# Stick-breaking attention: later key blocks summed on VectorE before the matmuls, and a later square for the head norm

## Chip, cores and metric

The kernel runs on one core of a Trainium2 chip. The metric is device time in microseconds (us): 2136.33 us, the median of 3 runs (2136.27 to 2136.56). The engines are called PE (TensorE matmul; PEld is its weight load), DVE (VectorE), ACT (ScalarE), POOL (GpSimd) and SP (the queue that issues the loads).

## The reference

Two transformer blocks run over 512 tokens of width 1024, all in float32. The part that the change touches is the attention of the second block, with 16 heads of 64:

```
q = rms_norm(q, q_gain); k = rms_norm(k, k_gain)      # per head
z = q @ k.T / sqrt(64)                                # masked: only keys s < t
log_1m = log_sigmoid(-z)                              # = -softplus(z)
rev_excl[s] = sum of log_1m over keys j with s < j < t
w = exp(log_sigmoid(z) + rev_excl);  o = w @ v
```

So every weight needs the sum of softplus(z) over all keys after its own. Besides, each of the seven mean-square norms (`rms_norm` over the 1024 rows) needs a sum over partitions.

## The kernel before

Tokens lie along the free axis, 512 wide, and features along the 128 partitions. Weights stream from HBM in chunks of 128x1024; ACT rounds each to a high half (L170), DVE subtracts to get the low half (L171), and each product is three matmuls: high x high, high x low, low x high (L193 to L195, function `mm3`). `split` does the same rounding for activations: ACT copies to fp32r (L188), DVE subtracts (L189). One such group of three 512-column matmuls is called a dense step here; for the value projection (`sv_tile`, L786 to L788) a dense step is six 256-column matmuls.

The attention takes two heads at a time, in eight passes called pair 0 to pair 7 here (`stick`). Scores are kept transposed: keys on partitions, queries on the free axis, only the part with query block >= key block. Side A is the first head, side B the second. The four key blocks of a head have 512, 384, 256 and 128 query columns, and `AT` packs both heads into five PSUM banks: A0 and B0 hold block 0 (512 columns), A1 and B1 hold block 1 (384) and block 3 (128), and Z2 holds block 2 of both sides (256 each). For each pair:

- `front` (L886 to L896): score matmuls, and one that adds the mask.
- ACT and DVE turn each bank z into softplus, bank after bank in the order A1, A0, Z2, B1, B0: absolute value (ACT L904, DVE L906), exp and log (ACT L910, L911), max and add (DVE L915). Then `split` makes the high and low part.
- `middle` (L925 to L931), once for each side: the matmuls that add minus the sum of later softplus onto z in PSUM. For each key block j a matrix with minus ones below and on the diagonal (`nlater`) goes onto block j itself, and a matrix of minus ones (`nones`) onto every earlier block; blocks of 128 columns in float32 (L925, two records each), the others with high and low part (L930, L931). They are called the first sums (side A) and the second sums (side B).
- `weights` (ACT L934): exp. `back` (PE L943): weights times values, for the pair before.

Between these stand dense steps of the projections for later pairs, so that PE has work while ACT and DVE work. `Flow` sets the order: `yield n` in `stick` pulls n dense steps from `sb_dense`, and each step advances a counter t; `F.at(d, fn)` emits a function's instructions d counts later; `tick` advances the counter without a dense step. `qk_tile` sends each projected q or k tile through a chain of this kind: evacuate (DVE L811), square (ACT L816), `NORM_LAG` counts later a float32 matmul over each head's 64 rows (`halves`, PE L822, called the head norm matmul), then `rsqrt` (ACT L232, L233, DVE L235 to L237) and a scale (DVE L828).

PE, ACT and SP run their instructions in the order in which the code emits them. The order on DVE and POOL is set when the program is built, by a scheduler with its own estimates, and is then fixed too: each engine works its list from top to bottom.

`Norm.total` (L257) sums the squares of the 1024 features with a matrix of ones: the sum of squares is split, and two fp32r matmuls of 512 columns run on it. It is called seven times, twice of them in `rstd_pair`.

Of the kernel before, what the change touches and what calls it, by code (L numbers as in the profile page):

```python
# [9 lines left out]
F32 = mybir.dt.float32  # L10
I32 = mybir.dt.int32
F32R = mybir.dt.float32r
AF = mybir.ActivationFunctionType
OP = mybir.AluOpType
PSUM = bass.MemoryType.PSUM

P = 128
S = 512
# [62 lines left out]
def block_kernel(ctx: ExitStack, tc: tile.TileContext, a, out):  # L81
    nc = tc.nc
    dve, act, pe, pool = nc.vector, nc.scalar, nc.tensor, nc.gpsimd

    consts = ctx.enter_context(tc.tile_pool(name="consts", bufs=1))
# [7 lines left out]
    def sl(dt=F32):  # L93
        return slots.tile([P, S], dt, name="sl", tag="sl")

    def bank():
        return psum.tile([P, S], F32, name="ps", tag="ps")
# [87 lines left out]
    def split(x):  # L185
        h = sl(F32R)
        l = sl(F32R)
        act.activation(h, x, AF.Copy)  # L188
        dve.tensor_tensor(l, x, h.bitcast(F32), op=OP.subtract)  # L189
        return h, l  # L190
# [25 lines left out]
    ones = cmat[:, 0:P]  # L216
    ident = cmat[:, P:2 * P]
    halves = cmat[:, 2 * P:3 * P]
    nlater = cmat[:, 3 * P:4 * P]
    nones = cmat[:, 4 * P:5 * P]  # L220
# [18 lines left out]
    class Norm:  # L239
# [13 lines left out]

        def total(self):
            ps = bank()
            for i, part in enumerate(split(self.acc)):
                pe.matmul(ps, ones_r, part, start=i == 0, stop=i == 1)  # L257
            return ps

        def rstd(self):  # L260
# [70 lines left out]
    for k in range(KD):  # L331
        xs.append(scaled_split(x[k], gain(G_N1, k)))
        wh, wl = split(lead[k])
        for n in range(4):
            c = slice(n * P, (n + 1) * P)
# [3 lines left out]
        norm.add(x[k])  # L339
    split_ahead()  # L340

    ones_r = consts.tile([P, P], F32R, name="ones_r")
    pool.tensor_copy(ones_r, ones)
    cc = consts.tile([P, KD], F32, name="cc")
    dve.tensor_tensor(cc, gains[:, G_NF * 8:G_NF * 8 + 8], gains[:, G_F1 * 8:G_F1 * 8 + 8], op=OP.mult)
    qg = consts.tile([P, 1], F32, name="qg")
# [15 lines left out]
    F = Flow()  # L362
# [338 lines left out]
    for m in range(KD):  # L701
# [3 lines left out]
        sa, sb = T.pop(T_GA + m), T.pop(T_GB + m)  # L705
# [9 lines left out]
    for m in [W_EARLY] + list(range(W_EARLY)) + list(range(W_EARLY + 1, KD)):  # L715
        if m < W_EARLY:
# [3 lines left out]
            ps = first[m][0]  # L720
        else:
            ps = bank()
# [46 lines left out]
    F = Flow()  # L769
# [31 lines left out]
    def qk_tile(n, which, g):  # L801
# [12 lines left out]
        def second(t):  # L814
            sq = sl()
            act.activation(sq, t, AF.Square)  # L816
            F.at(NORM_LAG, lambda: third(t, sq))

        def third(t, sq):
            pm = bank()  # L820
            state["bank_free"] = F.t + 8
            pe.matmul(pm, halves, sq, start=True, stop=True)  # L822
            F.at(2, lambda: fourth(t, pm))
# [37 lines left out]
    A0, A1, Z2, B1, B0 = range(5)  # L861
    AT = ({0: (A0, 0), 1: (A1, 0), 2: (Z2, 0), 3: (A1, 384)}, {0: (B0, 0), 1: (B1, 0), 2: (Z2, 256), 3: (B1, 384)})
# [6 lines left out]
    nlater_r = consts.tile([P, P], F32R, name="nlater_r")  # L869
    pool.tensor_copy(nlater_r, nlater)  # L870
    nones_r = consts.tile([P, P], F32R, name="nones_r")
# [3 lines left out]
    def stick():  # L875

        def front(n):

            q, k = Q[n], K[n]
            z = [bank() for _ in range(5)]
            started = set()
            for g, sb in ((0, 1), (1, 1), (0, 3), (1, 3), (0, 0), (1, 0), (0, 2)):
                b, c = AT[g][sb]
                pe.matmul(z[b][:, c:c + S - sb * P], k[HALF[g], sb * P:(sb + 1) * P], q[HALF[g], sb * P:],  # L886
                          start=b not in started, stop=True, skip_group_check=True)
                started.add(b)

            b, c = AT[1][2]  # L890
            pe.matmul(z[b][:, c:c + 2 * P], kz[(8 + n) % 3], q[:, 2 * P:], start=False, stop=True, skip_group_check=True)
            for b in (A1, A0, Z2, B1, B0):
                blocks = z[b].rearrange("p (a c) -> p a c", a=4)
                n_ = 1 if b in (A0, B0) else 2
                blocks = blocks[:, 0:1] if n_ == 1 else blocks[:, 0:3:2] if b == Z2 else blocks[:, 0:4:3]
                pe.matmul(blocks, ident_r, hidden_r[:, :n_ * P].rearrange("p (a c) -> p a c", a=n_), start=False,  # L896
                          stop=True, skip_group_check=True)
            return z

        def absolute(z, b):  # L900

            t = sl()
            if b in (A1, B1):
                act.activation(t, z[b], AF.Abs)  # L904
                return t
            dve.tensor_scalar(t.bitcast(I32), z[b].bitcast(I32), 0x7FFFFFFF, None, op0=OP.bitwise_and)  # L906
            return t

        def log_part(t):
            act.activation(t, t, AF.Exp, scale=-1.0)  # L910
            act.activation(t, t, AF.Ln, bias=1.0)  # L911

        def soft(t, z):

            dve.scalar_tensor_tensor(t, z, 0.0, t, op0=OP.max, op1=OP.add)  # L915

        def middle(z, sp, hl, g):
            for j in ((3, 1, 0, 2), (3, 1, 2, 0))[g]:
                bj, cj = AT[g][j]
                w = S - j * P  # L920
                for sb in range(j, -1, -1):
                    b, c = AT[g][sb]
                    dst = z[b][:, c + (j - sb) * P:c + (j - sb) * P + w]
                    if w == P:
                        pe.matmul(dst, nlater if j == sb else nones, sp[bj][:, cj:cj + w], start=False, stop=True,  # L925
                                  skip_group_check=True)
                        continue
                    hi, lo = hl[bj]
                    m = nlater_r if j == sb else nones_r
                    pe.matmul(dst, m, hi[:, cj:cj + w], start=False, stop=True, skip_group_check=True)  # L930
                    pe.matmul(dst, m, lo[:, cj:cj + w], start=False, stop=True, skip_group_check=True)  # L931

        def weights(z, t, b):
            act.activation(t[b], z[b], AF.Exp)  # L934

        def back(n, t):

            po = bank()
            for sb in range(4):
                for g in range(2):  # L940
                    b, c = AT[g][sb]
                    cv = (sb % 2) * 256 + (n % 2) * P + g * 64
                    pe.matmul(po[HALF[g], sb * P:], v[sb // 2][n // 2][:, cv:cv + 64], t[b][:, c:c + S - sb * P],  # L943
                              start=sb == 0, stop=sb == 3)
            pair = split(po)
            F.at(3, lambda: os_.__setitem__(n, pair))

        last = None
        for n in range(KD):
            while n not in K and F.pull(1):  # L950
                pass
            while n not in K:
                F.t += 1
                F.fire()
            z = front(n)
            F.tick(4)
            sp, hl = {}, {}
            order = (A1, A0, Z2, B1, B0)
            for t in range(6):

                for b in order[:2] if t == 0 else order[t + 1:t + 2]:
                    sp[b] = absolute(z, b)
                if t < 5:
                    log_part(sp[order[t]])
                if 1 <= t:
                    soft(sp[order[t - 1]], z[order[t - 1]])
                if 2 <= t < 5:
                    hl[order[t - 2]] = split(sp[order[t - 2]])
                yield 3 if t < 4 else 2
            middle(z, sp, hl, 0)  # L970
            F.tick(4)
            hl[B1] = split(sp[B1])
            yield 1
            hl[B0] = split(sp[B0])
            yield 3
            weights(z, sp, A1)
            weights(z, sp, A0)
            middle(z, sp, hl, 1)
            F.tick(2)
            for b in (B1, Z2, B0):  # L980
                weights(z, sp, b)
            yield 1
            if n:
                while F.t < state["bank_free"] and F.pull(1):
                    pass
                while v[1][(n - 1) // 2] is None and F.pull(1):
                    pass
                back(n - 1, last)
                F.tick(3)
            yield 2  # L990
            last = sp
        yield 7
        back(KD - 1, last)

    F.dense = sb_dense()
    for steps in stick():
        F.pull(steps)
# [7 lines left out]
    for m in [ne] + list(range(KD)):  # L1005
        if m == ne and xs[m] is not None:
            continue
        ps = bank()
        w = SBO_K[m] if m < ne else 0
# [22 lines left out]
ROPE_LAG = 10  # L1032
STACK_LAG = 5
BACK = 3
NORM_LAG = 4
SCALE_LAG = 8
VALUE_LAG = 4
SBO_K = (5, 5, 6, 6, 6)
# [94 lines left out]
```

## Time and profile before

| what | value |
|---|---|
| median of 3 runs | 2136.33 us |
| the profiled execution | 2135.5 us, its span 2133.6 us |
| PE busy | 2110.0 us (99% of the span) |
| DVE, ACT busy | 1090.8 us (51%), 840.8 us (39%) |
| mean granted PE clock | 0.997 of full speed |
| attention of the second block | about 1499 to 1744 us of the span |

Matmuls are pipelined: a record's duration overlaps the next, so the time that a matmul takes from PE is the distance between the starts of two, called its pitch here. On the other engines too an instruction often starts shortly before the one ahead has ended, so their cost in a row is also a pitch. A float32 matmul shows as two records.

### The profile page before, as it was taken

What the parts mean: (1) busy time and instruction counts of PE and PEld (TensorE: products, weight loads), DVE (VectorE), ACT (ScalarE), POOL (GpSimd) and SP (SyncE); (2) the same over time, 40 slices, a digit from 0 to 9 for tenths busy, and PEclk for the clock granted to TensorE, in tenths of its full rate; (3) what the DMA queues carried; (4) which work ended last, traced back from release to release, by engine and by line L of the source; (5) the groups of instructions that cost most, each with busy time, mean ns of one, the idle gap of its engine ahead of it and who ended that gap; (6) DMA issues with size and microseconds to landing.
All of it is one profiled execution on the core that took longest, in us unless ns stands there. A gap on an engine that the chain in (4) does not pass through costs nothing.

```text
span 2133.6 us, 24868 instructions
## 1 busy us (share of the span) xinstructions
PE 2110.0 (99%) x10022; PEld 1742.3 (82%) x10022; DVE 1090.8 (51%) x1607; ACT 840.8 (39%) x1319; POOL 14.4 (1%) x48
## 2 busy tenths in 40 slices
PE   8999999999999999999999999999999999999999
PEld 7888888887788888888887888888777878888887
DVE  6444344699954744444445444344766656444322
ACT  6222222366766542222233222223656644222210
POOL 0000000000000000000000000000000000000000
PEclk9999999999999999999999999999999999999999
DMA  5323333322212333332332223333111113323331
GB/s 173 104 97 99 92 101 109 102 89 75 72 55 65 119 99 99 99 99 82 101 97 96 92 96 99 92 91 98 58 51 58 35 55 128 97 92 97 97 116 54
DMA packets 58562, 193.55 MB, mean 91 GB/s; under 512 B 6928, under 2 KB 7568, under 8 KB 58448
## 3 DMA queue, kind: packets, MB, share of 16 engines
q1 hardware_dynamic: 56736, 188.67, 28.4%
q0 software_dynamic: 640, 2.10, 0.3%
q8 instruction: 78, 1.28, 0.2%
q10 hardware_dynamic: 1072, 1.21, 0.2%
q14 instruction: 36, 0.29, 0.0%
HBM read 189.20 MB, written 2.10 MB: 90 GB/s over the span
## 4 chain that ended last, share of the span: by engine, by line
PE 89%; DVE 6%; ACT 3%; issue 1%; DMA 1%; SPq 0%; ACTq 0%; DVEq 0%
PE ps L193 26%; PE ps L195 26%; PE ps L194 26%; DVE wl L171 1%; PE ps L943 1%; PE ps L886 1%; PE ps L574 1%; PE ps L931 1%; DVE sl L529 1%; PE ps L631 1%; DMA wraw<-in_f_in_dram 1%; PE ps L930 1%; ACT wh L170 1%; PE ps L562 1%; DVE m L527 1%
## 5 line engine op out<-in xcount | busy, mean ns | idle before, releaser
L193 PE MATMUL ps<-sl,wh 128*128 128x512 f32 x2672 | 1053.2, 394 | 0.0
L194 PE MATMUL ps<-sl,wh 128*128 128x512 f32 x2672 | 1041.7, 390 | 0.2
L195 PE MATMUL ps<-sl,wl 128*128 128x512 f32 x2672 | 1041.8, 390 | 0.0
L193 PEld LDWEIGHTS ps<-sl,wh 128*128 128x128 f32 x2672 | 502.6, 188 | 106.6 <-issue 6.0
L194 PEld LDWEIGHTS ps<-sl,wh 128*128 128x128 f32 x2672 | 502.8, 188 | 105.4 <-issue 2.9
L195 PEld LDWEIGHTS ps<-sl,wl 128*128 128x128 f32 x2672 | 502.4, 188 | 105.4
L170 ACT ACTIVATE wh<-wraw 128x1024 fp32r<-128x1024 f32 (+6 forms) x369 | 369.7, 1003 | 514.8 <-issue 248.8
L171 DVE TENSOR_TENSOR wl<-wraw,wh 128x1024 fp32r<-128x1024 f32 (+6 forms) x369 | 427.5, 1160 | 281.0 <-ACT wh L170 280.4
L188 ACT ACTIVATE sl<-sl 128x512 fp32r<-128x512 f32 x160 | 99.6, 627 | 393.4 <-DVE sl L301 387.5
L301 DVE TENSOR_TENSOR sl<-ps,sl 128x512 f32<-128x512 f32 x88 | 60.9, 692 | 270.2 <-PE ps L195 263.9
L189 DVE TENSOR_TENSOR sl<-sl 128x512 fp32r<-128x512 f32 x160 | 110.0, 689 | 69.8 <-ACT sl L188 69.3
L299 DVE TENSOR_TENSOR sl<-ps,sl 128x512 f32<-128x512 f32 x88 | 60.8, 691 | 140.1 <-PE ps L195 139.9
L251 ACT ACTIVATE sl<-x 128x512 f32<-128x512 f32 x42 | 25.8, 627 | 116.4 <-DVE x L324 97.7
L323 DVE SCALAR_TENSOR_TENSOR sl<-ps,sl 128x512 f32<-128x512 f32 x32 | 22.1, 692 | 80.0 <-PE ps L195 80.0
L300 ACT ACTIVATE sl<-sl 128x512 f32<-128x512 f32 x88 | 54.1, 614 | 9.2 <-DVE sl L299 9.2
L548 ACT ACTIVATE sl<-sl,mx 128x128 f32<-128x128 f32 (+3 forms) x64 | 35.7, 558 | 41.6 <-DVE mx L547 41.4
L555 ACT ACTIVATE sl<-sl,sm 128x128 f32<-128x128 f32 (+3 forms) x64 | 35.8, 560 | 25.2 <-DVE sm L554 15.1
L631 PE MATMUL ps<-sl 128*128 128x256 f32 (+2 forms) x176 | 43.4, 328 | 0.8 <-DVE mx L547 0.8
L252 DVE TENSOR_TENSOR sl<-sl 128x512 f32<-128x512 f32 x49 | 33.3, 690 | 18.0 <-ACT sl L251 17.5
L235 DVE SCALAR_TENSOR_TENSOR sl<-sl 128x512 f32<-128x512 f32 x23 | 15.9, 692 | 48.1 <-ACT sl L233 48.0
L631 PEld LDWEIGHTS ps<-sl 128*128 128x128 f32 x176 | 33.2, 189 | 8.6 <-DVE mx L547 1.2
L786 PE MATMUL ps<-wh,sl 128*128 128x256 f32 x128 | 37.8, 295 | 0.0
(143 smaller groups left out, 1338.0 us busy)
## 6 DMA issues: line engine op xcount, KB each, us to landing
wraw<-in_f_in_dram SPq DMA_DIRECT2D x172, 512.0 KB
wraw<-in_f_out_dram SPq DMA_DIRECT2D x64, 512.0 KB
wraw<-in_mix_t_dram SPq DMA_DIRECT2D x34, 512.0 KB
wraw<-in_f_out_dram SPq DMA_DIRECT2D x32, 384.0 KB
wraw<-in_sb_qk_dram SPq DMA_DIRECT2D x16, 512.0 KB
wraw<-in_br_dram SPq DMA_DIRECT2D x16, 256.0 KB
wraw<-in_w_out_dram SPq DMA_DIRECT2D x8, 512.0 KB
wraw<-in_sb_v_dram SPq DMA_DIRECT2D x8, 512.0 KB
```

Source lines behind the costliest of these rows:

```text
L170: act.activation(wh[:, :n], raw[:, :n], AF.Copy)
L171: dve.tensor_tensor(wl[:, :n], raw[:, :n], wh[:, :n].bitcast(F32), op=OP.subtract)
L188: act.activation(h, x, AF.Copy)
L189: dve.tensor_tensor(l, x, h.bitcast(F32), op=OP.subtract)
L193: pe.matmul(ps, wh, xh, start=start, stop=False)
L194: pe.matmul(ps, wh, xl, start=False, stop=False)
L195: pe.matmul(ps, wl, xh, start=False, stop=stop)
L299: dve.tensor_tensor(g, pg, rs, op=OP.mult)
L300: act.activation(g, g, AF.Silu)
L301: dve.tensor_tensor(g, pu, g, op=OP.mult)
L631: pe.matmul(ps[:, :n], q[:, i * P:(i + 1) * P], part[:, :n], start=x_ == 0, stop=x_ == 1)
L786: pe.matmul(dst, hh, wh[:, cl], start=kk == 0 and b == 0, stop=False)
```

## The change

Three things change. `Norm.total` does one float32 matmul on the unsplit sum. `NORM_LAG` goes from 4 to 6. In `stick`, a new function `suffix` adds up the softplus of later key blocks on DVE, in place, once own parts have been split: block 3 onto block 2's columns, and that onto block 1's; both results are split (ACT L922, DVE L923, 256 and 384 wide). `middle` then takes for each block its own part with `nlater` and one total of all later blocks with `nones`. The yields and ticks around the sums change with it.

```diff
         def total(self):
             ps = bank()
-            for i, part in enumerate(split(self.acc)):
-                pe.matmul(ps, ones_r, part, start=i == 0, stop=i == 1)
+            pe.matmul(ps, ones, self.acc, start=True, stop=True)
             return ps
...
-        def middle(z, sp, hl, g):
-            for j in ((3, 1, 0, 2), (3, 1, 2, 0))[g]:
...
+        def suffix(sp, hl, g, out):
+
+            b1, c2 = AT[g][1][0], AT[g][2][1]
+            two, one = sp[Z2][:, c2:c2 + 256], sp[b1][:, :384]
+            dve.tensor_tensor(two[:, P:], two[:, P:], sp[b1][:, 384:], op=OP.add)
+            dve.tensor_tensor(one[:, P:], one[:, P:], two, op=OP.add)
+            for s, w in ((two, 256), (one, 384)):
+                h, l = sl(F32R), sl(F32R)
+                act.activation(h[:, :w], s, AF.Copy)
+                dve.tensor_tensor(l[:, :w], s, h[:, :w].bitcast(F32), op=OP.subtract)
+                out.append((h[:, :w], l[:, :w]))
+
+        def middle(z, sp, hl, later, g):
+            def take(sb, m, m_r, at, parts):
+                b, c = AT[g][sb]
+                w = S - sb * P - at
+                for part in parts:
+                    pe.matmul(z[b][:, c + at:c + at + w], m if len(parts) == 1 else m_r, part, start=False, stop=True,
+                              skip_group_check=True)
+
+            last_block = sp[AT[g][3][0]][:, 384:]
+            for sb in ((3, 1, 0, 2), (3, 1, 2, 0))[g]:
+                b, c = AT[g][sb]
+                own = [last_block] if sb == 3 else [part[:, c:c + S - sb * P] for part in hl[b]]
+                take(sb, nlater, nlater_r, 0, own)
+            take(2, nones, None, P, [last_block])
+            take(1, None, nones_r, P, later[0])
+            take(0, None, nones_r, P, later[1])
...
                 if 2 <= t < 5:
                     hl[order[t - 2]] = split(sp[order[t - 2]])
+                if t == 4:
+                    suffix(sp, hl, 0, sums[0])
                 yield 3 if t < 4 else 2
-            middle(z, sp, hl, 0)
-            F.tick(4)
+            middle(z, sp, hl, sums[0], 0)
+            F.tick(3)
             hl[B1] = split(sp[B1])
             yield 1
+            suffix(sp, hl, 1, sums[1])
+            yield 2
             hl[B0] = split(sp[B0])
-            yield 3
+            yield 2
             weights(z, sp, A1)
             weights(z, sp, A0)
-            middle(z, sp, hl, 1)
+            middle(z, sp, hl, sums[1], 1)
...
-NORM_LAG = 4
+NORM_LAG = 6
```

PE's list, first sums of pair 2, before (`cmat` holds the float32 matrices, `nlater_r` and `nones_r` are their fp32r copies):

```order
L925 MATMUL ps<-sl,cmat 128x128 x4
L930 MATMUL ps<-sl,nlater_r 128x384
L931 MATMUL ps<-sl,nlater_r 128x384
L930 MATMUL ps<-sl,nones_r 128x384
L931 MATMUL ps<-sl,nones_r 128x384
L930 MATMUL ps<-sl,nlater_r 128x512
L931 MATMUL ps<-sl,nlater_r 128x512
L930 MATMUL ps<-sl,nlater_r 128x256
L931 MATMUL ps<-sl,nlater_r 128x256
```

Two more pairs of 256 columns on `nones_r` follow these rows. The same sums in the changed kernel, with the matmul that now follows them:

```order
L931 MATMUL ps<-sl,cmat 128x128
L931 MATMUL ps<-sl,nlater_r 128x384 x2
L931 MATMUL ps<-sl,nlater_r 128x512 x2
L931 MATMUL ps<-sl,nlater_r 128x256 x2
L931 MATMUL ps<-sl,cmat 128x128
L931 MATMUL ps<-sl,nones_r 128x256 x2
L931 MATMUL ps<-sl,nones_r 128x384 x2
L819 MATMUL ps<-sl,cmat 128x512
```

Two float32 matmuls and two of 256 columns (a high and a low part) are gone; the last four now read what `suffix` makes, and a head norm matmul (L819, L822 before) stands right behind. In pair 2's second sums (side B) the order of own blocks is 3, 1, 2, 0 as before, but block 0's 512-column pair now stands ahead of all `nones`.

DVE's list in pair 2 before, from the split of Z2 (`sl_11917`) over that of B1 (`sl_11933`) to that of B0 (`sl_11957`):

```order
L189 TENSOR_TENSOR sl_12006<-sl_11917,sl_12005 128x512
L235 SCALAR_TENSOR_TENSOR sl_12056<-sl_12053 128x512
L236 SCALAR_TENSOR_TENSOR sl_12056<-ps_12034,sl_12056 128x512
L237 SCALAR_TENSOR_TENSOR sl_12052<-sl_12056,sl_12053 128x512
L189 TENSOR_TENSOR sl_12063<-sl_11933,sl_12062 128x512
L828 SCALAR_TENSOR_TENSOR sl_11986<-sl_11986,gains_80,sl_12052 128x512
L189 TENSOR_TENSOR sl_12073<-sl_11957,sl_12072 128x512
```

One `rsqrt` and its scale lie among the three splits. The same place in the changed kernel, first from the split of Z2 (`sl_11906`) to that of B1 (`sl_11922`); A1 is `sl_11882`:

```order
L189 TENSOR_TENSOR sl_11981<-sl_11906,sl_11980 128x512
L912 SCALAR_TENSOR_TENSOR sl_11940<-ps_11858,sl_11940 128x512
L918 TENSOR_TENSOR sl_11906<-sl_11906,sl_11882 128x128
L918 TENSOR_TENSOR sl_11906<-sl_11906,sl_11922 128x128
L919 TENSOR_TENSOR sl_11882<-sl_11882,sl_11906 128x256
L923 TENSOR_TENSOR sl_11987<-sl_11906,sl_11986 128x256
L923 TENSOR_TENSOR sl_11991<-sl_11882,sl_11990 128x384
L235 SCALAR_TENSOR_TENSOR sl_12004<-sl_12001 128x512
L236 SCALAR_TENSOR_TENSOR sl_12004<-ps_11967,sl_12004 128x512
L237 SCALAR_TENSOR_TENSOR sl_12000<-sl_12004,sl_12001 128x512
L825 SCALAR_TENSOR_TENSOR sl_11904<-sl_11904,qg_335,sl_12000 128x512
L189 TENSOR_TENSOR sl_12045<-sl_11922,sl_12044 128x512
```

Side A's `suffix` and side B's first add lie behind the split of Z2, then a whole `rsqrt` with its scale. Then, on to the split of B0 (`sl_11940`):

```order
L923 TENSOR_TENSOR sl_12057<-sl_11906,sl_12056 128x256
L919 TENSOR_TENSOR sl_11922<-sl_11922,sl_11906 128x256
L923 TENSOR_TENSOR sl_12061<-sl_11922,sl_12060 128x384
L235 SCALAR_TENSOR_TENSOR sl_12074<-sl_12071 128x512
L236 SCALAR_TENSOR_TENSOR sl_12074<-ps_12042,sl_12074 128x512
L237 SCALAR_TENSOR_TENSOR sl_12070<-sl_12074,sl_12071 128x512
L794 TENSOR_SCALAR sl_12087<-ps_11960,rcol2_11109 128x256
L825 SCALAR_TENSOR_TENSOR sl_11969<-sl_11969,gains_80,sl_12070 128x512
L794 TENSOR_SCALAR sl_12087<-ps_11960,rcol2_11109 128x256
L189 TENSOR_TENSOR sl_12091<-sl_11940,sl_12090 128x512
```

The rest of side B's `suffix`, a second whole `rsqrt`, its scale and a value tile's evacuation now stand between the splits of B1 and B0. Before, one `rsqrt` stood there in all.

## Rows read from the trace of the kernel before

**Rows 1.** The page, part 1: busy time, share of the span, instructions

```profile
PE 2110.0 (99%) x10022; PEld 1742.3 (82%) x10022; DVE 1090.8 (51%) x1607; ACT 840.8 (39%) x1319; POOL 14.4 (1%) x48
```

**Rows 2.** PE's waits in all: total us, times, longest us

```profile
PE ps L822 <- ACT sl L816: 2.9, 2, 1.6
PE ps L257 <- DVE sl L189: 2.5, 2, 1.8
PE ps L257 <- ACT sl L188: 2.0, 1, 2.0
...
PE ps L931 <- DVE sl L189: 1.3, 3, 0.6
```

**Rows 3.** PE's timeline, pair 0: start us, us, line, shape, count

```profile
1518.33 0.39 PE L195 MATMUL ps<-sl,wl 128*128 128x512 f32 x1
1518.56 1.02 PE L822 MATMUL ps<-sl,cmat 128*128 128x512 f32 x2
...
1519.65 0.40 PE L194 MATMUL ps<-sl,wh 128*128 128x512 f32 x1
```

**Rows 4.** PE's timeline, pair 7: first sums, and where the second begin

```profile
1732.36 1.05 PE L925 MATMUL ps<-sl,cmat 128*128 128x128 f32 x8
1733.16 0.42 PE L930 MATMUL ps<-sl,nlater_r 128*128 128x384 f32 x1
1733.42 0.34 PE L931 MATMUL ps<-sl,nlater_r 128*128 128x384 f32 x1
...
1736.52 1.05 PE L925 MATMUL ps<-sl,cmat 128*128 128x128 f32 x8
```

**Rows 5.** PE's timeline around the two totals of rstd_pair

```profile
1123.31 0.63 PE L257 MATMUL ps<-sl,ones_r 128*128 128x512 f32 x2
...
1128.76 0.63 PE L193 MATMUL ps<-sl,wh 128*128 128x512 f32 x1
...
1131.62 0.40 PE L194 MATMUL ps<-sl,wh 128*128 128x512 f32 x1
```

**Rows 6.** Busy by engine there: stretch; PE, PEld, DVE, ACT, POOL; PEclk, DMA, GB/s

```profile
1129.00:1130.00 1.00, 1.00 (x3) 0.75 (x3) 1.00 (x2) 0.00 (x0) 0.00 (x0) 0.50 0.00 0
```

**Rows 7.** Groups by shape on DVE and ACT: count | busy us, mean ns | idle before

```profile
L171 DVE TENSOR_TENSOR wl<-wraw,wh 128x1024 fp32r<-128x1024 f32 x305 | 372.8, 1223 | 212.7 <-ACT wh L170 212.3
...
L547 DVE CUSTOM_DVE_ANT_0 sl<-ps,sl 128x128 f32<-128x128 f32 x8 | 2.2, 277 | 0.0
...
L170 ACT ACTIVATE wh<-wraw 128x1024 fp32r<-128x1024 f32 x305 | 320.9, 1054 | 426.5 <-issue 216.3 <-PE ps L194 183.0 <-DMA wraw<-in_f_in_dram 10.3
...
L170 ACT ACTIVATE wh<-wraw 128x384 fp32r<-128x384 f32 x2 | 1.0, 508 | 0.0
```

**Rows 8.** Timeline, pair 2, around its first sums, ACT and DVE

```profile
1587.59 0.67 ACT L232 ACTIVATE sl<-ps,epst 128x512 f32<-128x512 f32 x1
...
1588.83 1.14 ACT L188 ACTIVATE sl<-sl 128x512 fp32r<-128x512 f32 x2
1588.96 0.69 DVE L235 SCALAR_TENSOR_TENSOR sl<-sl 128x512 f32<-128x512 f32 x1 [0.47 <-ACT sl L233]
...
1591.02 0.68 DVE L189 TENSOR_TENSOR sl<-sl 128x512 fp32r<-128x512 f32 x1
1591.62 0.74 DVE L828 SCALAR_TENSOR_TENSOR sl<-sl,gains 128x512 f32<-128x512 f32 x1
1592.29 0.68 DVE L189 TENSOR_TENSOR sl<-sl 128x512 fp32r<-128x512 f32 x1
...
1592.89 0.87 DVE L797 TENSOR_SCALAR sl<-ps,rcol 128x256 f32<-128x256 f32 x2
```

**Rows 9.** Timeline, pair 3: its first ACT work, its split of Z2, first sums

```profile
1603.34 0.60 ACT L904 ACTIVATE sl<-ps 128x512 f32<-128x512 f32 x1 [4.11 <-PE ps L896]
...
1614.10 0.61 ACT L188 ACTIVATE sl<-sl 128x512 fp32r<-128x512 f32 x1
...
1614.58 1.05 PE L925 MATMUL ps<-sl,cmat 128*128 128x128 f32 x8
```

More of the change, by code (lines that the diff above doesn't have):

```diff
@@ L340, in block_kernel @@
     split_ahead()
-    ones_r = consts.tile([P, P], F32R, name="ones_r")
-    pool.tensor_copy(ones_r, ones)
     cc = consts.tile([P, KD], F32, name="cc")
@@ L915, in soft @@
             dve.scalar_tensor_tensor(t, z, 0.0, t, op0=OP.max, op1=OP.add)
-        def middle(z, sp, hl, g):
-            for j in ((3, 1, 0, 2), (3, 1, 2, 0))[g]:
[L919 to L931, printed above, removed]
+        def suffix(sp, hl, g, out):
[23 more added lines that the diff above has]
+            take(0, None, nones_r, P, later[1])
         def weights(z, t, b):
@@ L956, in stick @@
             F.tick(4)
-            sp, hl = {}, {}
+            sp, hl, sums = {}, {}, ([], [])
             order = (A1, A0, Z2, B1, B0)
```

## The prediction

> **What bounds the kernel now.** I read four views: the page, the list of waits, the timeline of PE, and the timelines of DVE and ACT around the sums. PE is busy for 99% of the span, DVE and ACT for about half or less [rows 1], so time is won on PE's own list, or lost where PE waits for one of the others. The reader is to see that PE's waits in the places touched are few: 2.9 us for the square before the head norm matmul, 2.5 and 2.0 us before the totals, 1.3 us for low parts in the sums [rows 2]. That is 8.7 us; all other gain must come from PE work that goes. And half-busy engines say nothing on order: a low part that stands late in DVE's list is late, however idle DVE is on average. So the second half of the working follows lists, with durations from rows.
>
> **Pitches.** A float32 matmul of 512 columns costs PE 0.86 us: from its start to the second dense matmul behind it 1.09 us pass, less 0.23 for the one between [rows 3]. So a dense step of three is 0.68 us, and by columns a 384-wide matmul 0.17, a 256-wide 0.12, a narrow dense step of the value projection 0.72. On DVE and ACT, 1024 columns take 1.22 and 1.05 us, 128 columns on DVE 0.28, 384 on ACT 0.51 [rows 7]; between these lie 0.41 and 0.55 us for 256 and 384 on DVE, 0.40 for 256 on ACT (estimates from these rows). In a row each costs about 0.1 less.
>
> **What PE saves in the sums.** Before, one side's sums take 2.80 us: 4.16 us from the first to the second sums of pair 7, less two dense steps [rows 4]. In this, four float32 matmuls of 128 columns take 0.80 and the first fp32r matmul behind them 0.26 in place of 0.17. After: two float32 (0.40), that 0.09 twice, own blocks 0.46 + 0.34 + 0.24, later totals 0.24 + 0.34: 2.20 us. Saved 0.6 us, sixteen times, with rounding 9.3 us.
>
> **The totals.** In rstd_pair, PE goes from the first total to the next dense matmul in 5.45 us [rows 5], because the second total's split stands behind the first rsqrt on ACT and DVE. Two float32 matmuls without a split take 1.72: 3.7 us saved. Behind these waits the granted clock is 0.50 of full speed, the lower level of 1.2 GHz, after PE had done one short matmul between two idle stretches of 2.0 and 1.8 us [rows 2, 6]; the seven matmuls up to 1131.62 take 2.86 us in place of 1.59 [rows 5]. With the waits this goes too: 1.3 us. The first total of the kernel loses its 0.7 us wait (the rest of the 2.5 [rows 2]) and pays 0.41 (0.86 against two at 0.23): 0.3 us saved. The other four have no wait and pay 0.41 each: 1.6 us. What the totals give is 3.7 + 1.3 + 0.3 - 1.6 = 3.7 us. The bounds are 2 (clock recovers anyway, rsqrt comes later behind the matmul) and 5. The constant `ones_r` made by POOL costs nothing either way.
>
> **The waits that go as such.** The head norm matmul's 2.9 us and the sums' 1.3 us [rows 2]: I take them as gone and count below every wait that the new lists give in the same places. Gains so far: 9.3 + 3.7 + 4.2 = 17.2 us.
>
> **What the sums now wait for.** In the first sums PE now reads, last of all, the low part of block 1's later total, 2.03 us after they begin (0.29 + 0.34 + 0.46 + 0.24 + 0.29 + 0.24 + 0.17). In the second sums the low part of B0 is wanted 1.1 us after the beginning (0.29 + 0.34 + 0.24 + 0.23); before it stood last, 2.5 us after it.
>
> Pair 2, times from the start of ACT's copy of Z2. Copy to 0.6; on DVE low part to 1.3, max-add of B0 to 1.9, two 128-wide adds to 2.3, the 256-wide add to 2.7; ACT's copies 2.2 to 2.6 and 2.8 to 3.3; DVE's last subtraction 3.3 to 3.9. When do the sums begin? In pair 3 the copy starts 10.8 us after the first ACT work, the sums 11.2 us after it [rows 9]. In pair 2 the new PE list has ten dense steps, six narrow ones and a head norm matmul, 1.0 us more than pair 3's fourteen and two, and on ACT a square more but a wait for DVE less; so they begin about 1.65 after the copy and want the last part at 3.7: a wait of 0.2, end at 4.1. Behind them stands the head norm matmul. Its square on ACT comes after Ln and Exp of the rsqrt before (1.24 us from 3.2 [rows 8]), so it ends at 5.1: a wait of 1.0. With 0.86 and five narrow steps the second sums begin at 9.6 and want B0 at 10.7. Meanwhile DVE: first rsqrt from 4.6, 2.06 us, scale 0.67, split of B1 0.6 [rows 8], to 7.9; suffix add to 8.7; ACT's 384-wide copy to 9.2, then Ln and Exp of the second rsqrt to 10.5; DVE rsqrt 2.06, scale 0.67, two evacuations 0.87 [rows 8], and only then the split of B0, to 14.8. A wait of 4.1 us. Pair 2 loses 5.3 us, pair 4 with the same lists as much.
>
> Pair 3: the sums begin 0.5 after the copy [rows 9] and want the last part at 2.5; it comes at 3.9: 1.4. With head norm and five steps the second sums begin at 8.4 and want B0 at 9.5. ACT has side B's last copy until 6.2, then a weight chunk (1.0), Ln and Exp to 8.4; DVE rsqrt 2.06, evacuation 0.6, scale 0.67, split: 12.6. A wait of 3.1. Together 4.5; pair 5 has a shorter chunk, 3.6. Pair 0 has only one rsqrt ahead of B0's split: 0.3 and 1.9. In pair 1 B0's split stands ahead of the rsqrt and Z2's copy 1.4 us before the sums: nothing. Pair 6 has no rsqrt among the splits: 0.4. In pair 7 the projections' dense steps have run out, since each pair now pulls 24 and before 23: fourteen stand before its first sums and none between first and second. First 0.9; then B1 and B0 are late by 2.2 in all. The four steps ran earlier, so they cost nothing in themselves.
>
> Sum of new waits: 2.2 + 0 + 5.3 + 4.5 + 5.3 + 3.6 + 0.4 + 3.1 = 24.4 us. The operations that no row shows are the 128- and 256-wide adds and narrow copies. If they cost half as much or half as much again, each pair's first sums shift by about 0.5 us and the second by 0.5: 16 to 32 us over the eight pairs. I take the middle, which follows the rows nearest in width.
>
> **The clock.** In pairs 2 and 4 PE stands idle for some 3.5 us at a stretch before B0's low part, right behind two shorter stops. The one row of this kind shows 1.3 us lost behind 3.7 us of waits [rows 5, 6]. I add 1.3 twice, 2.6 us; bounds 0 and, if pairs 3 and 5 (3.1 and 2.6 us) do the same, 5.2.
>
> **Sum.** Against the profiled execution's 2135.5 us: + 24.4 + 2.6 - 17.2 = + 9.8, or 2145.3; the median of the runs is 0.8 us above that execution, so 2146 us.
>
> **Rivals.**
> (1) Faster: B0's low part is not the late one. The place is DVE's list between the splits of B1 and B0, and the point is 1.1 us after the second sums begin. If Ln and Exp of the second rsqrt come some 4 us earlier than I chain them, only the waits in the first sums and the one before head norm stay, 6.4 us, and the kernel needs 17.2 - 6.4 = 10.8 us less: 2125.5 us. For it: the average load is low [rows 1], and the wait for low parts was only 1.3 us with an rsqrt among the splits as well. Against it: then B0 was wanted 1.4 us later, and one rsqrt less lay ahead.
> (2) About the same: the waits come but at their lower bound, 16 us, without loss of clock: 17.2 - 16 = 1.2 us less, 2135 us; with 21, 2140.
> (3) Worse: the clock falls behind the stops of pairs 3 and 5 too, as in [rows 6], and the waits are at 28: 2136.3 + 28 + 5.2 - 17.2 = 2152 us. The Trainium skill, "TensorE: Matmul & The Clock Gate" (Part 1, What's actually happening), says in my words that throttled is the default and activity is what releases the clock; by that rule each of these stops would cost a slow stretch after it, which is this rival. The trace agrees at one place, the row with 0.50 [rows 6].
> (4) The later square does not do what it says: the wait of 2.9 us before the head norm matmul moves rather than goes. I already have 1.0 us each in pairs 2 and 4; with 2.9 in full it is 0.9 more, 2147, and no case of its own.
>
> **How the numbers follow.** A measurement here tells a change from none at about 0.2%, 4.3 us. Forecast (2141 to 2151): 0.53. Rival 3 (over 2151): 0.13. Rival 2 (2132 to 2141): 0.19, nearly all within 0.2%. Rival 1 (below 2132): 0.15. So slower 0.66, same 0.18, faster 0.16. The range from 2131 to 2154 leaves out most of rival 1 and the tail of rival 3.
>
> **What would show it.** Right: PE's waits list has the sums' line waiting for DVE L189, longest some 4 us, and about 24 us for the sums' line and the head norm together; in pairs 2 and 4 DVE's split of B0 starts right behind a scale and an evacuation while PE is idle; the totals' line has no wait, and PE goes through the two of rstd_pair in 1.7 us. Wrong: waits on the sums' line under 12 us in all, or late `suffix` parts (DVE L923) as the main releaser in place of L189. The saved work is wrong if the first sums without waits do not take 2.2 us.

## The result, and the profile after

The changed kernel takes 2147.97 us (median of 4 runs, 2146.71 to 2148.86) beside 2136.39 for the kernel before (4 runs): a ratio of 1.0056, with a 95% interval of 1.0043 to 1.0069. It is slower by 11.6 us; 2146 was forecast, with a range of 2131 to 2154. The profiled execution has 2146.71 us, with a span of 2144.9; it is the fastest of the four and was granted 0.997 of full clock in the mean, the other three, which have no trace, 0.994.

First the page's busy times, which answer to [rows 1]:

```profile
PE 2110.6 (98%) x9926; PEld 1735.1 (81%) x9926; DVE 1110.7 (52%) x1664; ACT 850.0 (40%) x1344; POOL 14.4 (1%) x47
```

PE executes 96 matmuls fewer and is as long busy, in a span that is 11.3 us longer: what was saved has come back as time between matmuls. The list of PE's waits (total us, times, longest) says where; it answers to [rows 2]. L819 is now the head norm matmul, L813 its square, L922 and L923 the suffix's copies and low parts:

```profile
PE ps L931 <- DVE sl L189: 12.1, 6, 3.2
...
PE ps L931 <- ACT sl L188: 3.2, 4, 1.1
...
PE ps L819 <- ACT sl L813: 1.4, 2, 0.7
PE ps L931 <- ACT sl L922: 1.4, 3, 0.6
...
PE ps L931 <- DVE sl L923: 0.6, 4, 0.2
```

The totals' line is gone from this list. In its place the sums wait for L189 and L188, the split: six times for its low part, up to 3.2 us. Pair 2 shows the longest. PE's timeline there (start us, us, line, shape, count, idle before and what ended it), second sums:

```profile
1586.16 0.39 PE L931 MATMUL ps<-sl,cmat 128*128 128x128 f32 x2
1586.31 0.83 PE L931 MATMUL ps<-sl,nlater_r 128*128 128x384 f32 x4
1587.65 0.49 PE L931 MATMUL ps<-sl,nlater_r 128*128 128x512 f32 x1 [0.51 <-ACT sl L188]
1591.35 0.80 PE L931 MATMUL ps<-sl,nlater_r 128*128 128x512 f32 x1 [3.21 <-DVE sl L189]
...
1593.44 0.41 PE L783 MATMUL ps<-wh,sl 128*128 128x256 f32 x1
```

And DVE's timeline of the same microseconds, which ends with the low part of B0 that PE wants (it answers to [rows 8]):

```profile
1587.11 0.69 DVE L235 SCALAR_TENSOR_TENSOR sl<-sl 128x512 f32<-128x512 f32 x1 [0.68 <-ACT sl L233]
1587.84 0.69 DVE L236 SCALAR_TENSOR_TENSOR sl<-ps,sl 128x512 f32<-128x512 f32 x1
1588.56 0.69 DVE L237 SCALAR_TENSOR_TENSOR sl<-sl 128x512 f32<-128x512 f32 x1
1589.17 0.48 DVE L794 TENSOR_SCALAR sl<-ps,rcol 128x256 f32<-128x256 f32 x1
1589.57 0.74 DVE L825 SCALAR_TENSOR_TENSOR sl<-sl,gains 128x512 f32<-128x512 f32 x1
1590.22 0.48 DVE L794 TENSOR_SCALAR sl<-ps,rcol 128x256 f32<-128x256 f32 x1
1590.62 0.68 DVE L189 TENSOR_TENSOR sl<-sl 128x512 fp32r<-128x512 f32 x1
```

Read the two together. B0's high part is there at 1587.6, when PE uses it. DVE is by then in a chain of an rsqrt, two evacuations and a scale, 3.5 us from 1587.11 to 1590.62, and only then subtracts; PE has nothing to do from 1588.1 until the subtraction is done. DVE itself is about half busy over the span.

ACT's timeline shows why that rsqrt is so late:

```profile
1585.31 0.52 ACT L922 ACTIVATE sl<-sl 128x384 fp32r<-128x384 f32 x1 [2.93 <-DVE sl L919]
1585.74 0.67 ACT L232 ACTIVATE sl<-ps,epst 128x512 f32<-128x512 f32 x1
1586.44 0.63 ACT L233 ACTIVATE sl<-sl 128x512 f32<-128x512 f32 x1
1586.98 0.61 ACT L188 ACTIVATE sl<-sl 128x512 fp32r<-128x512 f32 x1
```

Side B's `suffix` is part of the chain: ACT stands idle for 2.93 us before its 384-wide copy (L922), until DVE has made the last add (L919, behind the first rsqrt in its list), and the rsqrt's Ln and Exp (L232, L233) and B0's own copy (L188) come behind that copy in ACT's list. The prediction chained it so.

Where nothing is late the new sums are as short as they were meant to be. In pair 1 the second sums start at 1553.06 and the next dense matmul at 1555.15: 2.09 us, where [rows 4] gave 2.80 by subtraction (to the next matmul, 1735.13, it is 2.77):

```profile
1553.06 0.38 PE L931 MATMUL ps<-sl,cmat 128*128 128x128 f32 x2
1553.19 1.31 PE L931 MATMUL ps<-sl,nlater_r 128*128 128x384 f32 x6
1554.34 0.38 PE L931 MATMUL ps<-sl,cmat 128*128 128x128 f32 x2
1554.48 0.83 PE L931 MATMUL ps<-sl,nones_r 128*128 128x256 f32 x4
1555.15 0.39 PE L193 MATMUL ps<-sl,wh 128*128 128x512 f32 x1
```

The totals of rstd_pair, beside [rows 5]: from 1124.46 to about 1126.2, 1.7 us (the second dense matmul less its pitch of 0.23), in place of 5.45, and no fall of the clock follows:

```profile
1124.46 1.88 PE L256 MATMUL ps<-sl,cmat 128*128 128x512 f32 x4
1125.77 0.80 PE L193 MATMUL ps<-sl,wh 128*128 128x512 f32 x1
1126.41 0.40 PE L194 MATMUL ps<-sl,wh 128*128 128x512 f32 x1
```

It falls instead behind the stops of pairs 2, 3 and 4, as in [rows 6]. The stretches behind pair 2's (us; PE busy and count; granted clock; DMA):

```profile
1591.00:1592.00 1.00, 0.65 (x2) 0.64 0.00 0
1592.00:1593.00 1.00, 1.00 (x6) 0.50 0.00 0
1593.00:1594.00 1.00, 1.00 (x6) 0.50 0.00 0
1594.00:1595.00 1.00, 1.00 (x7) 0.65 0.00 0
```

Half clock is the lower level, 1.2 GHz. What is missing to 1.00 adds up to 1.7 us here, and to as much behind pairs 3 and 4: some 5.1 us in all, a little less where PE was still idle.

Side by side, the time of all sixteen sums, each from its first matmul to the next of another line (so with a wait before the head norm matmul where that follows at once), is 46.6 us before and 62.5 after. At 2.77 and 2.09 us a side without waits it would be 44.3 and 33.4.

### The profile page after: what moved, and what is told of

Its sections match the earlier page's. It is cut to its first block, busy times and chain, and to the rows that moved or that the text cites. A ratio compares the mean times of both kernels' runs of the same rounds, so it can differ in the third digit from the quotient of the medians.

```text
span 2144.9 us, 24779 instructions
## 1 busy us (share of the span) xinstructions
PE 2110.6 (98%) x9926; PEld 1735.1 (81%) x9926; DVE 1110.7 (52%) x1664; ACT 850.0 (40%) x1344; POOL 14.4 (1%) x47
## 4 chain that ended last, share of the span: by engine, by line
PE 86%; DVE 8%; ACT 4%; issue 1%; DMA 0%; DVEq 0%
PE ps L193 26%; PE ps L194 26%; PE ps L195 26%; DVE wl L171 1%; PE ps L953 1%; PE ps L883 1%; PE ps L931 1%; DVE sl L526 1%; DVE sl L189 1%; ACT sl L907 1%; ACT sl L908 1%; PE ps L571 1%; DVE m L524 1%; PE ps L628 1%; ACT wh L170 1%
## 5 line engine op out<-in xcount | busy, mean ns | idle before, releaser
L188 ACT ACTIVATE sl<-sl 128x512 fp32r<-128x512 f32 x153 | 96.0, 627 | 387.2 <-DVE sl L300 383.3
L189 DVE TENSOR_TENSOR sl<-sl 128x512 fp32r<-128x512 f32 x153 | 105.5, 690 | 68.3 <-ACT sl L188 67.7
L299 ACT ACTIVATE sl<-sl 128x512 f32<-128x512 f32 x88 | 54.0, 614 | 12.2 <-DVE sl L298 12.1
L552 ACT ACTIVATE sl<-sl,sm 128x128 f32<-128x128 f32 (+3 forms) x64 | 35.9, 560 | 25.3 <-DVE sm L551 14.8
L252 DVE TENSOR_TENSOR sl<-sl 128x512 f32<-128x512 f32 x49 | 33.3, 691 | 18.0 <-ACT sl L251 17.5
L783 PE MATMUL ps<-wh,sl 128*128 128x256 f32 x128 | 39.9, 312 | 0.0
L931 PE MATMUL ps<-sl,nlater_r 128*128 128x384 f32 (+2 forms) x96 | 24.5, 371 | 15.4 <-DVE sl L189 12.1
```

What stands on the lines that cost most here:

```text
L299: act.activation(g, g, AF.Silu)
L931: pe.matmul(z[b][:, c + at:c + at + w], m if len(parts) == 1 else m_r, part, start=False, stop=True, skip_group_check=True)
```

## The experiments

Each kernel below the first row was timed beside the kernel before on the same chip; the latter's median there lay between 2135.56 and 2136.28 us.

| kernel | us | against before |
|---|---|---|
| the change | 2148.0 | +11.6 |
| totals alone | 2132.3 | -3.7 |
| later square alone | 2132.2 | -3.8 |
| both, without the new sums | 2127.7 | -8.2 |
| new sums alone | 2144.4 | +8.4 |
| change, B0 split ahead of the scale | 2139.6 | +3.7 |
| change, B0 split ahead of the rsqrt | 2124.7 | -11.3 |
| the same, lag of four | 2135.7 | -0.3 |
| B0 ahead, suffix earlier | 2123.9 | -12.1 |
| the same, lag of seven | 2129.4 | -6.9 |
| B0 ahead, lag of eight | 2126.8 | -9.5 |
| B0 ahead, new sums on side B alone | 2120.9 | -14.7 |

**The parts alone.** The kernel before with the totals' edit only:

```diff
-            for i, part in enumerate(split(self.acc)):
-                pe.matmul(ps, ones_r, part, start=i == 0, stop=i == 1)
+            pe.matmul(ps, ones, self.acc, start=True, stop=True)
```

> The kernel before with only the totals changed (one float32 matmul in place of split and two). My sum gave 3.7 us less, so 2132.7; what the changed kernel's trace has shown since (2.4 us gained up to pair 0's front, and one total more after the attention) points to 2 to 3, so 2133.4 to 2134.4, with no wait left before rstd_pair's totals and 1.7 us from the first to the next dense matmul. Rival: the split only kept PE's order, the float32 matmuls and a later rsqrt take back what the wait gave: 2136, no difference.

Measured: 2132.33 us (2131.35 to 2132.70), 3.7 less, as the prediction's sum had it, and more than the expectation corrected it to. The rival falls.

The kernel before with `NORM_LAG = 6` only:

> The kernel before with only the later square (head norm matmul six steps behind instead of four). My theory: the 2.9 us before the head norm matmul go, but every rsqrt starts 1.4 us later, and behind it B0's split; with the old sums B0 is wanted 2.5 us after they begin and nothing is added up on DVE, so it is late by about 1 us in pairs 2 and 4 alone: 2134 to 2137. Rival: the later square alone makes the rsqrt late for B0, and is what slowed the changed kernel: 2141 or more.

Measured: 2132.18 us (2131.29 to 2133.36), 3.8 less, better than forecast: of the waits before the head norm matmul 0.2 us are left in the list, and of the sums' 0.9. With the old sums the later rsqrt harms nothing.

The two together, without the new sums:

> The kernel before with the float32 totals and the later square, without the new sums. If the two small parts are independent, as my theory has it (3.7 and 3.8 us less, measured one at a time): 2128.5 (2127.5 to 2129.5). Rival, that they share a gain (a fall of the clock counted in both): 2130 to 2132. The new sums in the changed kernel then cost the difference to 2148, and with B0's split ahead they give the difference to 2124.7.

Measured: 2127.74 us (2126.96 to 2128.44). They add up, within 0.8 us: the first theory holds.

The new sums with the old totals and a lag of four:

> The changed kernel with the old totals and the old lag of four steps: the sums alone. My theory: PE's list is 9.3 us shorter, but B0's split still stands behind the second rsqrt, which begins 1.4 us earlier than in the changed kernel: new waits of about 19 us in place of 24, the old 2.9 before the head norm stay: 2142 to 2146. Rival, that the lag is what makes B0 late: no long wait for B0's low part is left, 2126 to 2130.

Measured: 2144.39 us (2142.59 to 2144.78). The time was forecast, the place was not: the rival's condition held (no long wait for B0's low part), and its time did not. PE's waits in that kernel (L822 is the head norm matmul, L934 the sums):

```profile
PE ps L822 <- ACT sl L816: 11.3, 5, 3.6
...
PE ps L934 <- DVE sl L189: 2.0, 3, 0.9
...
PE ps L934 <- ACT sl L188: 1.1, 1, 1.1
```

At four steps PE stops 11.3 us for the square and hardly for B0. The square is late for a like reason; in pair 2 it waits for DVE to evacuate its tile (L811), which stands behind the whole first rsqrt in DVE's list (L235 to L237 from 1586.22):

```profile
1588.28 0.68 DVE L811 TENSOR_TENSOR sl<-ps,sl 128x512 f32<-128x512 f32 x1
1588.99 0.63 ACT L816 ACTIVATE sl<-sl 128x512 f32<-128x512 f32 x1 [2.81 <-DVE sl L811]
```

While PE stops there (3.65 us in pair 2) DVE catches up: B0's subtraction starts at 1595.43, before the second sums do (1595.78). At six steps the square is nearly in time (1.4 us) and the stop comes later, at B0 (15.3 us with L188). With the new sums the lag alone so moves the stop and does not remove it.

**The place of B0's split.** One dense step earlier (`yield 1`, split, `yield 3` in place of `yield 2`, split, `yield 2`):

> The changed kernel with the split of B0 one dense step earlier: in pairs 2 to 5 its low part then stands behind the whole of the second rsqrt on DVE, but ahead of the scale (0.67 us) and of the evacuations (0.4 to 0.6 each). My theory, that B0's low part is late by all that stands ahead of it in DVE's list: the waits shrink by what is passed, about 1.5 us in pairs 2 and 4 and 1.2 in pairs 3 and 5, 5.4 us in all, 2142.5 (2139 to 2144 with a fall of the clock less). Rival, that the suffix adds or ACT's copy are what it waits for: nothing changes, 2146 to 2149; rival that any place ahead of the scale is early enough: 2125 to 2130.

Measured: 2139.64 us (2137.31 to 2141.01), in the forecast. L189's total falls from 12.1 to 6.7, the longest from 3.2 to 1.8:

```profile
PE ps L931 <- DVE sl L189: 6.7, 6, 1.8
```

The wait shrinks by what is passed, 1.45 us in pairs 2 and 4. That much is shown to be DVE's order alone, since the waits for ACT's copy (L188, 3.2 us) stay. Of the rest it says nothing: the rsqrt and, through ACT, the suffix are still ahead of the split.

Ahead of the second rsqrt too, and of the second side's suffix, on ACT and on DVE (these two were not tried apart):

```diff
             hl[B1] = split(sp[B1])
+            hl[B0] = split(sp[B0])
             yield 1
             suffix(sp, hl, 1, sums[1])
-            yield 2
-            hl[B0] = split(sp[B0])
-            yield 2
+            yield 4
```

> The changed kernel with the split of B0 made right behind that of B1, ahead of the suffix adds of the second side and of the second rsqrt; PE's list is the same. My theory: the sums' waits for B0's low part in pairs 2 to 5 (3.2, 2.8, 3.2, 2.4 us in the trace, each some 0.3 more from start to start) and in pair 0 (1.1 and 0.2) go, and the clock's falls behind them (about 1.3 each, three in the profiled run): 15 to 18 us less than the changed kernel, 2130 to 2133, faster than before. Rival, that the suffix's own parts are what the second sums lack: these waits move to the suffix's low parts and 2143 to 2148 stays.

Measured: 2124.68 us (2124.14 to 2126.98), 23.3 less than the changed kernel with the same list on PE; ratio to before 0.9950 (0.9938 to 0.9963). The rows for L189 and L188 are gone, and the sums' waits are these:

```profile
PE ps L931 <- ACT sl L922: 1.4, 3, 0.6
...
PE ps L931 <- DVE sl L923: 0.6, 4, 0.2
```

What DVE then does in pair 2, where the second sums begin at 1583.96:

```profile
1581.71 1.28 DVE L189 TENSOR_TENSOR sl<-sl 128x512 fp32r<-128x512 f32 x2
...
1585.16 0.69 DVE L235 SCALAR_TENSOR_TENSOR sl<-sl 128x512 f32<-128x512 f32 x1 [0.68 <-ACT sl L233]
```

The rsqrt comes no earlier than in the changed kernel, 1.2 us after the second sums begin (there 0.95), and now does no harm; both splits are done by 1583.0. So the cause is shown: the place of B0's split behind suffix and rsqrt. The gain was forecast 5 us too small. From their first matmul to the next of another line, the second sums of pairs 0 and 2 to 5 are 17.5 us shorter (some 2 of it half clock) where 14 were listed as waits, pair 7 (left out of the expectation) gives 1.3 more, and a fall of the clock cost 1.7, not 1.3.

The same with the lag of four:

> The kernel with B0's split ahead, with the old lag of four steps before the head norm matmul. The run of the sums alone with that lag waited 11.3 us there, in five places, the longest 3.6. My theory: the later square and the place of B0's split are two separate needs; those waits come back and B0's do not: 9.9 us more listed than at six steps, some 0.35 more at each of the further three, and one or two falls of the clock: 2135 to 2139. Rival, that B0's split ahead also clears the way for the square: 2124 to 2128.

Measured: 2135.66 us (2134.24 to 2136.88), in the forecast, and the wait is where it was said:

```profile
PE ps L819 <- ACT sl L813: 11.4, 5, 3.6
```

With the new sums the later square is worth 11 us if B0's split is out of the way, and with the split where the change puts it, it costs 7 (2148.0 against 2144.4 less the totals' 3.7; that last sum takes the totals to add up here too, which was not tried).

**What is left.** Z2's split and the first side's suffix made at the fourth of the six stages, not at the fifth (three dense steps earlier by the `yield 3` between; the expectation says two):

```diff
-                if 2 <= t < 5:
+                if 2 <= t < 4:
                     hl[order[t - 2]] = split(sp[order[t - 2]])
-                if t == 4:
+                if t == 3:
+                    hl[Z2] = split(sp[Z2])
                     suffix(sp, hl, 0, sums[0])
```

> The kernel with B0's split ahead, and besides it Z2's split and the suffix adds of the first side two dense steps earlier, as soon as Z2's softplus is there, ahead of B0's Exp and Ln on ACT. My theory: the waits that are left in the first sums (seven, 2.0 us listed, with some 0.35 each from start to start 4.4 us) go, the two before the head norm stay or shrink a little: 2119.5 to 2122. Rival, that B0's softplus, now 1.5 us later on ACT, makes the second sums late instead: 2124 to 2130.

Measured: 2123.87 us (2123.77 to 2125.43), 0.8 less, within the spread of both: a miss. The rival's reason does not hold either: the second sums of pairs 2 to 5 still take 2.1 us. The first sums' waits go nearly all, and PE, sooner at the head norm matmul, waits there five times in place of two:

```profile
PE ps L819 <- ACT sl L813: 3.5, 5, 0.9
...
PE ps L931 <- ACT sl L188: 0.8, 1, 0.8
```

So the lag was raised, to seven with the earlier suffix and to eight without it:

> The kernel with B0's split and the first side's suffix both ahead, with the head norm matmul seven steps behind instead of six. There the waits that the earlier suffix took from the first sums had come back before the head norm (3.5 us in five places, the longest 0.9). My theory, that a wait goes for good only when each reader on PE's list is put behind its own producer: one dense step of 0.68 to 0.72 us covers nearly all of the 3.5, with 0.35 more at each: 2119 to 2120.5. Rival, that the rsqrt, later again, makes something else late (the scaled rows of the next pair, or bank order): 2123 to 2126.

> The kernel with B0's split ahead, the suffix where the change put it, and the head norm matmul eight steps behind. My theory: the two waits before the head norm (1.4 us listed) go, the seven in the first sums (2.0) stay, and the later rsqrt costs nothing, since no split stands behind it any more: 2122.5 to 2124. Rival, that each two steps more cost what two cost in the changed kernel: 2127 or more.

Measured: 2129.42 us (2127.98 to 2130.25) and 2126.76 us (2125.86 to 2127.49): both slower than at six, and both forecasts were missed. Of the rivals' reasons the bank order is borne out. At seven a new wait stands behind the head norm matmul:

```profile
1584.08 0.39 PE L783 MATMUL ps<-wh,sl 128*128 128x256 f32 x1 [2.04 <-DVE sl L236]
```

L783 is the first matmul of a value projection, which takes a new bank; L236 is DVE reading the head norm's sum in the rsqrt. The projection uses nothing that the rsqrt computes. By the code all they share is the banks that go round: it waits for one that the rsqrt still reads, twice, in pairs 2 and 4. These two stops are 4.1 of the 5.5 us; in pair 7 the sums take 1.0 us more and the clock falls in them. At eight the wait for the bank is 0.6 us, but the order in pair 0 has changed: its first sums take 5.76 us in place of 2.56, with 2.2 listed, and the clock falls right behind them (1.7 us missing to 1.00 from 1525 to 1529). Against that stand the first sums of pairs 2 to 5, about 1.2 us shorter in each. What makes the 2.1 us of difference was not tried.

Last, B0's split ahead, and the first sums as before the change (`middle`'s old loop for side A, no suffix for it):

> The kernel with B0's split ahead, but the later blocks of side A summed in matmuls as before; only side B is added up on VectorE. Without waits a side takes 2.77 us in the old form and 2.08 in the new, but from start to end (with the wait before the head norm matmul, where that follows at once) side A took 3.4 to 3.7 in pairs 2 to 5 of the kernel with both sides new. My theory: adding up saves only where PE has other work until the sums are there; eight second sums at 0.69 us less than in the run without new sums (2127.7) give 2122.2, and the first sums have no wait but the one of pair 2 (0.9 us): 2121.5 to 2123. Rival, that the saved matmuls count on side A as well, whatever is listed as a wait: 2125.5 or more, slower than with both sides new (2124.7).

Measured: 2120.86 us (2120.09 to 2121.34), ratio 0.9931 (0.9917 to 0.9944): 15 us faster than before, 27 faster than the change, and 0.6 below the forecast's range. All sixteen sums, measured as above, take 39.3 us, against 43.6 with both sides new. In PE's timeline of pair 2 the head norm matmul (L819) now follows the first sums (L951, L956) at once, 2.77 us after they begin, and the second sums take 2.09:

```profile
1575.92 1.05 PE L951 MATMUL ps<-sl,cmat 128*128 128x128 f32 x8
...
1578.69 1.02 PE L819 MATMUL ps<-sl,cmat 128*128 128x512 f32 x2
...
1583.13 0.39 PE L931 MATMUL ps<-sl,cmat 128*128 128x128 f32 x2
...
1585.22 0.28 PE L783 MATMUL ps<-wh,sl 128*128 128x256 f32 x1
```

From 1504 to 1723 us, which is nearly all of the attention, PE is busy without a gap:

```profile
1504.00:1723.00 219.00, 219.00 (x1292) 1.00 0.16 49
```

So side A's longer sums are the cheaper ones: they need no result that comes late, and with them the square has its time.

## Why the prediction was right

The time (2146 for 2148), the mechanism and its place were right, and the sizes nearly. That the time is so close is in part luck: savings were taken 2.6 us too small and costs 5.1 us too small, which cancels in half. Term by term:

| term | predicted us | measured us |
|---|---|---|
| sums shorter | -9.3 | -10.9: 16 x (2.77 - 2.09) |
| totals, with the clock behind them | -3.7 | -3.7, alone |
| old waits gone | -4.2 | -5.2: 2.9 before the head norm, 2.3 in the sums from start to start |
| new waits | +24.4 | about +27: 62.5 - 33.4, less some 2 at half clock |
| clock | +2.6 | +5.1: three falls of 1.7 |
| sum | +9.8 | +12.3; the two spans differ by 11.3 |

About 1 us stays unassigned. A side without waits takes 2.09 us, where the prediction summed 2.20; its own 0.6 us, sixteen times, would be 9.6, not 9.3.

**The chain.** In pair 2 the prediction counts from ACT's copy of Z2, which starts at 1576.54: first sums at +1.65, second sums at +9.6, end of B0's low part at +14.8. The trace has 1578.23, 1586.16 and 1591.30: +1.7, +9.6, +14.8. Durations from rows of other places, chained in list order, gave these times to a tenth.

**The new waits by pair.** Each side's time less 2.09, first and second, beside the prediction: pair 0 2.5 (2.2), pair 1 0.3 (0), pair 2 6.5 (5.3), pair 3 5.5 (4.5), pair 4 5.7 (5.3), pair 5 4.0 (3.6), pair 6 0.6 (0.4), pair 7 4.0 (3.1). The order among them is right and each forecast is too low. In pairs 2 and 3 half clock is most of the difference (1.0 and 0.9 us); without it all come within 0.4 us but pair 7's.

**The mis-sized term: the clock.** The prediction took two falls at 1.3 us, behind pairs 2 and 4. In the profiled execution there were three, pair 3 with them, and each cost 1.7; that its upper bound of 5.2 is nearly the value is luck, four falls at 1.3 for three at 1.7. The three slower executions, at 0.994, must have had more half clock; where is not known. That is rival 3's mechanism in part. The rule it names (the Trainium skill, "TensorE: Matmul & The Clock Gate", Part 1, What's actually happening: throttled is the default, and activity releases the clock) fits pairs 2, 3 and 4, but pair 5 shows that not every stop of this kind costs.

**The sign that was not met.** "About 24 us for the sums' line and the head norm together" in the list of waits: it holds 18.7, and its longest wait is 3.2, not some 4. The waits were not smaller; the list does not hold all of them. In pair 2's first sums nothing is listed and 0.72 before the head norm matmul, yet from 1578.23 they take 3.38 us to that matmul, 1.29 too many. The Trainium skill, "Perfetto Trace Analysis", section "Tensor Engine Instruction (MATMUL, LD_WEIGHTS)", says that the end of such an instruction in a profile is estimated, not observed. The trace agrees: a matmul of 512 columns is shown with 0.39 us at a pitch of 0.23, and idle time is counted only from such an end. The other signs were met: in pair 2 DVE's split of B0 starts right behind a scale and an evacuation while PE is idle, L923 holds only 0.6 us, and the totals take 1.7 us without a wait.

**The rivals.** Rival 1 (B0's low part not late, 2125.5 us) is what the kernel with B0's split ahead runs: 2124.7. Its price was right; its condition, that the second rsqrt leave B0 alone, does not hold in the changed kernel. Rival 2 (waits at the lower bound) falls: the sums lost about 27 us, not 16 to 21. Rival 4 got no case of its own, and there the prediction saw only half. The later square does do what it says (11.3 us before the head norm matmul at four steps, 1.4 at six), but what it takes away there comes back at B0. That the old lag would meet the new sums with 11 us of waits was not foreseen; so the later square is no small extra here, but what the new sums need once B0's split is out of the way.

## What to carry to other kernels

Work taken from the engine that bounds pays only where that engine has something else to do until the result is there. Look at what the results' producer stands behind in its own list, not at how busy that engine is: one line moved ahead of a suffix and a 3.5 us chain was worth 23 us, and giving up half of the saving (side A) another 4. When a wait is removed, ask which reader is next on the bounding engine's list; here it went from the head norm matmul to B0 and, with a longer lag, to a bank.

## What the runs showed of the hardware

Stops of one length, and the clock fell after one and not after the other. In the changed kernel pair 5's second sums start again after 2.44 us listed; in the run of the sums alone pair 0's head norm matmul after 2.43. PE's row after the stop in the changed kernel, and a stretch behind it (the granted clock is third from the end):

```profile
1695.32 0.50 PE L931 MATMUL ps<-sl,nlater_r 128*128 128x512 f32 x1 [2.44 <-DVE sl L189]
```

```profile
1696.00:1697.00 1.00, 1.00 (x10) 1.00 0.00 0
```

The same two of the sums alone:

```profile
1528.33 2.07 PE L822 MATMUL ps<-sl,cmat 128*128 128x512 f32 x2 [2.43 <-ACT sl L816]
```

```profile
1529.00:1530.00 1.00, 1.00 (x3) 0.50 0.00 0
```

PE was busy right up to both stops. What tells them apart was not tried; a stop's listed length alone does not say whether the clock falls.

A bank can be what a matmul waits for: with the head norm seven steps behind, a projection that has no part in the rsqrt stood 2.04 us until DVE had read the head norm's sum. That the bank is what the two share is read from the code; no run had another number of banks.
